# Finishing a LayerNorm with two fused VectorE operations in place of three engines' work, in a hybrid DeltaNet and retention layer

## Chip, core and metric

The kernel runs on one core of one Trainium2 chip. The core's engines are TensorE (PE in the profile, its weight loads PEld), VectorE (DVE), ScalarE (ACT), GpSimd (POOL) and SyncE (SP), which issues every transfer of this kernel. The metric is the time of one execution on the device, in microseconds (us). Three runs of the kernel before took 1587.22 to 1591.74 us, with a median of 1589.14.

## What is computed

The reference is one layer of a diffusion backbone over 1152 tokens of 1024 channels: 128 context tokens and 1024 latent tokens. A mixer with two head groups (gated DeltaNet and retention) is followed by an output projection, a first LayerNorm over the residual, a modulated second LayerNorm, a squared-ReLU MLP and a last LayerNorm. The lines that matter here:

```python
def layer_norm(x, w=None, b=None, eps=1e-6):
    xf = x.astype(jnp.float32)
    mu = jnp.mean(xf, -1, keepdims=True)
    var = jnp.mean(jnp.square(xf - mu), -1, keepdims=True)
    y = (xf - mu) * lax.rsqrt(var + eps)
    if w is not None:
        y = y * w.astype(jnp.float32) + b.astype(jnp.float32)
    return y.astype(x.dtype)
...
        x = layer_norm(ALPHA * x + g1 * y, ln1_w[l], ln1_b[l])
        h = layer_norm(x) * (1.0 + sc2) + sh2
        f = jnp.einsum('btf,fd->btd', jnp.square(jax.nn.relu(jnp.einsum('btd,df->btf', h, w_ff1[l]) + b_ff1[l])),
                       w_ff2[l]) + b_ff2[l]
        x = layer_norm(ALPHA * x + g2 * f, ln2_w[l], ln2_b[l])
```

The first of these norms, with `ln1_w` and `ln1_b`, is the one that the change touches. It is called the first norm below; the plain norm of the next line is the second norm.

## The kernel before

Tokens are worked on in nine tiles of 128 rows. Matrix products are made in three passes: each operand is split into a high part (a cast on ScalarE, line 160) and a low part (a subtraction on VectorE, line 161), and TensorE adds up high by high, high by low and low by high.

The program goes through the input projection, the two scans, the output projection, the MLP's first product, its second product, and the last norm. The change lies in the output projection. Its steps are written as small functions, and a string gives their order (`OPS`, then `FFS`); each letter is a function and each number a tile's place in the order (4, 5, 3, 6, 7, 8, 2, 1, 0). A mark such as `^2500` lets a step's instructions count as that much earlier when the program is ordered. Instructions are put into each engine's queue by a scheduler from priorities and its own times, and each engine then works through its queue in order.

- `L` is `op_load` (line 1067 on): it loads the mixer's output of one tile into `wr` tiles, of which there are two, and splits it (lines 160 and 161).
- `M` is `op_mm`: TensorE multiplies by the output weights (line 1011). For the first six tiles half of the product was made earlier, so `op_mm` has 24 matmuls of 512 columns there and 48 for the last three. VectorE multiplies the PSUM result by the gate (line 1092). For the first six tiles the sum is added to the residual by VectorE for one half and by GpSimd for the other (line 1094); for the last three VectorE does it in one operation (line 1096).
- `A` is `norm1`, the first norm: `stats` (VectorE, lines 245 to 249, then a power on GpSimd for the reciprocal root, line 157), `act_normalise` (a 128x1 product on GpSimd, line 254, and scale and shift on ScalarE, line 255), times the weight on VectorE (line 1103), plus the bias on GpSimd (line 1104), and a store to X1 in device memory, which is read again only near the end of the kernel.
- `B` is `norm2`, the second norm, from the same tile in SBUF: `stats` and `act_normalise` into one of two `n2` tiles.
- `C` is `modulate`: TensorE transposes `n2` (line 1120), ScalarE modulates it out of PSUM into one of two `tmp` tiles (line 1124), the split follows, and `tmp` is stored to HX.
- `F` in `FFS` runs a part of the MLP's first product early (line 194), from the chunks of tokens that are ready.

The small tile `mv` of `stats` holds, in its columns, the mean, the variance plus epsilon, minus the mean (column 2, by line 248) and the reciprocal root (column 3, by line 157). `act_normalise` overwrites column 2 with minus the mean times the root. In the trace the first six tiles of `norm1` appear under the name hL and the last three under r, `mv` as lnmv, and `n2` as n.

Of the kernel before, what the change touches and what calls it, by code (L numbers as in the profile page):

```python
# [12 lines left out]
ALU = mybir.AluOpType  # L13
# [67 lines left out]
def layer_kernel(ctx: ExitStack, tc: tile.TileContext, A, O):  # L81
    nc = tc.nc
    V, S, G, T = nc.vector, nc.scalar, nc.gpsimd, nc.tensor

    def dma(out, in_):
        nc.sync.dma_start(out=out, in_=in_)
# [18 lines left out]
    def pool(name, side="left", **kw):  # L105
        p = tc.tile_pool(name=name, bufs=1, reuse_waits="tile", **(kw or dict(side=side)))
        e = ExitStack()
        p = e.enter_context(p)
        return p, e.close
# [43 lines left out]
    def sb(pool, shape, tag, bufs=1, dt=F32):  # L153
        return pool.tile(shape, dt, tag=tag, name=tag, bufs=bufs)

    def rsqrt(pool, out, in_, n):
        G.tensor_tensor(out=out, in0=in_, in1=ex[:, 0, 0:n], op=ALU.pow)  # L157
# [82 lines left out]
    def stats(pool, x, n, eps):  # L240

        h = n // 512
        st = sb(pool, [128, 2, 6], "lnst", 2)
        for j in range(h):
            V.bn_stats(out=st[:, j, :], in_=x[:, 512 * j:512 * j + 512])  # L245
        mv = sb(pool, [128, 4], "lnmv", 4)
        V.bn_aggr(out=mv[:, 0:2], in_=st[:, 0:h, :])
        V.tensor_scalar(out=mv[:, 2:3], in0=mv[:, 0:1], scalar1=-1.0, scalar2=None, op0=ALU.mult)
        V.tensor_scalar(out=mv[:, 1:2], in0=mv[:, 1:2], scalar1=eps, scalar2=None, op0=ALU.add)  # L249
        rsqrt(pool, mv[:, 3:4], mv[:, 1:2], 1)  # L250
        return mv

    def act_normalise(pool, out, x, mv):
        G.tensor_tensor(out=mv[:, 2:3], in0=mv[:, 2:3], in1=mv[:, 3:4], op=ALU.mult)
        S.activation(out=out, in_=x, func=AF.Identity, scale=mv[:, 3:4], bias=mv[:, 2:3])
# [801 lines left out]
    op, close_op = pool("op")  # L1057
# [3 lines left out]
    l1w = sb(op, [128, 1024], "l1w")  # L1061
    dma(l1w, A["ln1_w"].to_broadcast([128, 1024]))
    l1b = sb(op, [128, 1024], "l1b")
# [35 lines left out]
    def norm1(i):  # L1099
        t = ORDER[i]  # L1100
        r = rt[i]
        act_normalise(op, r, r, stats(op, r, 1024, 1e-6))
        V.tensor_tensor(out=r, in0=r, in1=l1w, op=ALU.mult)
        G.tensor_tensor(out=r, in0=r, in1=l1b, op=ALU.add)
        dma(X1[128 * t:128 * t + 128], r)

    def norm2(i):
# [23 lines left out]
    n2 = {}  # L1131
    HX = dram.tile([1024, NT], F32, name="HX")
    run(OPS, dict(L=op_load, M=op_mm, A=norm1, B=norm2, C=modulate))
    close_ow()

# [29 lines left out]
    def ff1_early(i):  # L1165
# [3 lines left out]
        ff1_chunk(early[f], f, c)  # L1169

    run(FFS, dict(A=norm1, B=norm2, C=modulate, F=ff1_early))
    close_op()
    close_psum()
# [382 lines left out]
```

## Time and profile before

| | |
|---|---|
| median of three runs | 1589.14 us |
| the profiled execution's own time | 1597.36 us |
| its span, first to last instruction | 1595.5 us |
| TensorE matmuls, busy | 1507.1 us, 94% |
| VectorE, busy | 1057.4 us, 66% |
| ScalarE, busy | 724.6 us, 45% |
| GpSimd, busy | 333.4 us, 21% |
| mean granted TensorE clock | 0.977 |

Durations of single instructions come from one profiled execution. The page of the profile gives the busy time of each engine, the span in 40 slices, and the chain of work that ended last. The trace behind it also answers with timelines of one engine (start, duration, engine, line, operation, result and operands, and in brackets the idle time before it and what ended it), with tables of windows, and with groups of instructions: their total, the mean in ns, and the idle time just before them. PE's busy time is modelled from pipelined matmuls, so a full row does not mean that they run at their peak.

### The profile page before, as it was taken

To read this page: it belongs to the slowest core of one execution; us is meant where nothing else is said; L and a number is where in the kernel's file an instruction comes from. 1 tells how busy PE (TensorE), PEld (TensorE's weight loads), DVE (VectorE), ACT (ScalarE), POOL (GpSimd) and SP (SyncE) were. 2 spreads that over 40 slices of the span, in tenths; PEclk is the share of its full clock that TensorE was granted. 3 is DMA by queue.
4 is the path that set the end of the run, shared out by engine and by line. 5 is a ranking of instruction groups with operands and counts; after the bars stand their busy time and mean duration, and the time that the engine had idled before them with its cause. 6 is when DMAs were issued, how large, how long until landed. Compare 5 with 4: busy or idle time off the path is not lost.

```text
span 1595.5 us, 26235 instructions
## 1 busy us (share of the span) xinstructions
PE 1507.1 (94%) x9597; PEld 1328.6 (83%) x9597; DVE 1057.4 (66%) x2045; ACT 724.6 (45%) x1562; POOL 333.4 (21%) x328
## 2 busy tenths in 40 slices
PE   4899999899999999999798999999999999999997
PEld 2697676898898989987687999999998788888885
DVE  4415424568795788657894576656666887867887
ACT  4522312564564464352457565445554453443411
POOL 2201021211112022100541035556553000000000
PEclk9799999999999999999898999999999999999998
DMA  9233556332323123454345944443347989878511
GB/s 347 74 82 83 172 157 200 77 78 70 82 49 102 37 58 108 122 163 161 104 152 158 292 154 139 154 155 128 125 139 260 333 281 315 290 237 284 169 54 66
DMA packets 227378, 247.81 MB, mean 155 GB/s; under 512 B 35956, under 2 KB 161889, under 8 KB 227121
## 3 DMA queue, kind: packets, MB, share of 16 engines
q1 hardware_dynamic: 227249, 246.13, 48.5%
q8 instruction: 76, 1.25, 0.3%
q14 instruction: 53, 0.43, 0.1%
HBM read 185.72 MB, written 56.15 MB: 152 GB/s over the span
## 4 chain that ended last, share of the span: by engine, by line
PE 51%; DVE 10%; issue 4%; ACT 3%; DMA 2%; POOL 2%; SPq 0%; DVEq 0%; POOLq 0%; ACTq 0%
PE d L1252 18%; PE m L1416 14%; PE mm L194 7%; PE d L194 3%; PE p L1416 2%; DVE lnst L245 2%; PE c L900 1%; PE c L891 1%; PE c L884 1%; DVE qk L638 1%; PE co L915 1%; PE co L914 1%; DVE wl L161 1%; DVE acc L1491 1%; POOL lnmv L157 1%
## 5 line engine op out<-in xcount | busy, mean ns | idle before, releaser
L194 PE MATMUL mm<-hH,wh 128*128 128x384 f32 x696 | 247.4, 356 | 2.0 <-ACT raw L634 2.0
L194 PE MATMUL mm<-hL,wh 128*128 128x384 f32 x696 | 246.6, 354 | 0.0
L194 PE MATMUL mm<-hH,wl 128*128 128x384 f32 x696 | 245.7, 354 | 0.0
L161 DVE TENSOR_TENSOR wl<-wr,wh 128x512 fp32r<-128x512 f32 (+1 forms) x149 | 126.8, 855 | 118.3 <-ACT wh L160 109.4
L1416 PE MATMUL m<-vh,sh 128*128 128x512 f32 x460 | 180.6, 393 | 3.4 <-DVE af L1308 3.0
L1416 PE MATMUL m<-vl,sh 128*128 128x512 f32 x460 | 179.8, 393 | 1.4 <-DVE vl L161 1.3
L1416 PE MATMUL m<-vh,sl 128*128 128x512 f32 x460 | 179.6, 391 | 0.4 <-DVE sl L161 0.4
L194 PEld LDWEIGHTS mm<-hH,wh 128*128 128x128 f32 x696 | 133.9, 192 | 7.3 <-ACT raw L634 2.2
L194 PEld LDWEIGHTS mm<-hL,wh 128*128 128x128 f32 x696 | 133.5, 192 | 5.5 <-issue 4.1
L194 PEld LDWEIGHTS mm<-hH,wl 128*128 128x128 f32 x696 | 133.4, 192 | 4.9 <-issue 3.7
L160 ACT CAST wh<-wr 128x512 fp32r<-128x512 f32 (+1 forms) x149 | 88.9, 613 | 78.8 <-PE mm L194 52.2
L1252 PE MATMUL d<-sh,wl 128*128 128x288 f32 x416 | 122.9, 295 | 0.5 <-DVE wl L161 0.5
L1252 PE MATMUL d<-sh,wh 128*128 128x288 f32 x416 | 122.7, 295 | 0.6 <-ACT wh L160 0.6
L1252 PE MATMUL d<-sl,wh 128*128 128x288 f32 x416 | 122.6, 295 | 0.0
L160 ACT CAST sh<-ar 128x512 fp32r<-128x512 f32 x103 | 63.8, 619 | 94.1 <-PE m L1416 46.1
L1416 PEld LDWEIGHTS m<-vh,sh 128*128 128x128 f32 x460 | 86.7, 189 | 22.9 <-issue 3.8
L157 POOL TENSOR_TENSOR lnmv<-lnmv,ex 128x1 f32<-128x1 f32 x36 | 22.0, 612 | 396.4 <-DVE lnmv L249 379.4
L1416 PEld LDWEIGHTS m<-vl,sh 128*128 128x128 f32 x460 | 86.5, 188 | 20.9 <-DVE vl L161 2.1
L1416 PEld LDWEIGHTS m<-vh,sl 128*128 128x128 f32 x460 | 86.8, 189 | 19.1 <-DVE sl L161 0.8
L161 DVE TENSOR_TENSOR sl<-ar,sh 128x512 fp32r<-128x512 f32 x103 | 70.7, 688 | 33.6 <-ACT sh L160 27.6
L1252 PE MATMUL d<-hH,wh 128*128 128x288 f32 x312 | 91.5, 294 | 0.0
L160 ACT CAST vh<-br 128x512 fp32r<-128x512 f32 x103 | 63.8, 619 | 48.9 <-DVE br L1380 32.2
(394 smaller groups left out, 3677.1 us busy)
## 6 DMA issues: line engine op xcount, KB each, us to landing
br<-in_w_ff_dram SPq DMA_DIRECT2D x168, 256.0 KB
ar<-HS SPq DMA_DIRECT2D x91, 256.0 KB
HS<-hL SPq DMA_DIRECT2D x65, 256.0 KB
wm<-in_w_mod_dram SPq DMA_DIRECT2D x32, 512.0 KB
wr<-in_w_in_dram SPq DMA_DIRECT2D x56, 256.0 KB
af<-HX SPq DMA_DIRECT2D x20, 576.0 KB
wm<-in_w_mod_dram SPq DMA_DIRECT2D x8, 1024.0 KB
w3h<-in_w_ff_dram SPq DMA_DIRECT2D x13, 512.0 KB
```

What stands on the lines that cost most here:

```text
L157: G.tensor_tensor(out=out, in0=in_, in1=ex[:, 0, 0:n], op=ALU.pow)
L160: S.copy(out=pool_hi, in_=src)
L161: V.tensor_tensor(out=pool_lo, in0=src, in1=pool_hi.bitcast(F32), op=ALU.subtract)
L194: T.matmul(p[:, 0:384], x[:, k % 4, :], y[c][:, k, :], start=(k == 0 and a == 0), stop=(k == 7 and a == 2),)
L245: V.bn_stats(out=st[:, j, :], in_=x[:, 512 * j:512 * j + 512])
L638: V.scalar_tensor_tensor(out=y, in0=raw[:, tap:tap + 1156], scalar=vec2[:, 12 * tap + ct:12 * tap + ct + 1], in1=y, op0=ALU.mult, op1=ALU.add,
L884: T.matmul(p[:, 0:128], qk[:, 0, off(n):off(n) + 128], old, start=True, stop=True)
L891: T.matmul(p[:, 0:128], UP[:, m_, 0, :], r, start=True, stop=True)
L900: T.matmul(p[:, 0:128], kt[:, n, :], y2, start=True, stop=True)
L914: T.matmul(p[:, 128:256], qk[:, 1, off(n):off(n) + 128], old, start=True, stop=True)
L1252: T.matmul(p[:, q, :], w[x][:, k, :], hs[y][:, k, CH * q:CH * q + CH], start=(k == 0 and a == 0), stop=(k == 3 and a == 2),)
L1416: T.matmul(p, x[i], w[j], start=(first and a == 0), stop=(last and a == 2))
```

## The change

The first norm no longer calls `act_normalise`. After `stats`, one VectorE operation adds minus the mean and multiplies by the weight, and a second one multiplies by the reciprocal root and adds the bias. The 128x1 product on GpSimd, the ScalarE pass, the VectorE product and the GpSimd addition of the first norm are gone; the statistics, the power on GpSimd and the store to X1 stay. The second norm is as it was.

```diff
     def norm1(i):
         t = ORDER[i]
         r = rt[i]
-        act_normalise(op, r, r, stats(op, r, 1024, 1e-6))
-        V.tensor_tensor(out=r, in0=r, in1=l1w, op=ALU.mult)
-        G.tensor_tensor(out=r, in0=r, in1=l1b, op=ALU.add)
+        mv = stats(op, r, 1024, 1e-6)
+        V.scalar_tensor_tensor(out=r, in0=r, scalar=mv[:, 2:3], in1=l1w, op0=ALU.add, op1=ALU.mult)
+        V.scalar_tensor_tensor(out=r, in0=r, scalar=mv[:, 3:4], in1=l1b, op0=ALU.mult, op1=ALU.add)
         dma(X1[128 * t:128 * t + 128], r)
```

## The prediction

> **What bounds the kernel now.** I read the page first, then the chain of waits, then the engines' timelines in the stretch that the chain led to, and last a table of windows. The page gives TensorE 94% of the span, so a change on three other engines can only matter where TensorE stands still. The first `norm1` starts its statistics near 757 us and the last of its work is over by 874 us, so these are the windows I asked for:
>
> ```profile
> core 0: us, PE busy (x) PEld busy (x) DVE busy (x) ACT busy (x) POOL busy (x), PEclk, DMA share, GB/s
> 756.00:874.00 118.00, 100.73 (x481) 86.17 (x480) 86.97 (x154) 67.80 (x133) 46.58 (x51) 0.93 0.42 134
> 779.00:787.00 8.00, 0.07 (x1) 0.07 (x2) 7.80 (x11) 4.65 (x11) 5.03 (x4) 0.65 0.47 145
> 779.00:838.00 59.00, 49.55 (x229) 41.27 (x230) 53.65 (x91) 33.88 (x66) 28.04 (x31) 0.91 0.48 150
> 838.00:874.00 36.00, 28.40 (x151) 26.69 (x150) 16.61 (x30) 28.43 (x64) 5.95 (x8) 0.90 0.48 152
> 874.00:1217.00 343.00, 341.81 (x2475) 341.11 (x2473) 216.93 (x250) 186.76 (x296) 154.37 (x113) 1.00 0.50 168
> ```
>
> TensorE lacks 17.3 us of the 118 in this stretch, 8 of them in one piece, and from 874 on it is busy 341.8 of 343 us. What is won before 874 should therefore reach the end one for one, unless a later transfer has a time of its own. In the piece of 59 us VectorE is busy 53.65, which is 91%: it stands next in line as a bound, and the change puts work on it. TensorE's own waits add up to the same 17.2:
>
> ```profile
> PE s L1120 <- ACT n L255: 8.2, 1, 8.2
> PE d L194 <- ACT tmp L1124: 3.8, 1, 3.8
> PE c L1120 <- ACT tmp L1124: 3.7, 1, 3.7
> PE co L1120 <- DVE r L1092: 1.5, 1, 1.5
> ```
>
> The chain of waits shows how the longest one comes about. Here `norm1` of one tile holds up `norm2` of the tile ahead of it, whose transposes TensorE has next in its queue:
>
> ```profile
> 770.88 0.19 POOL lnmv L254
> ...
> 774.25 2.41 POOL hL L1104
> 776.66 0.97 POOL lnmv L157
> ...
> 777.92 1.25 ACT hL L255
> 779.20 1.24 DVE hL L1103
> ...
> 780.50 0.77 POOL hL L1104
> ...
> 782.80 1.58 POOL hL L1094
> 784.38 0.96 POOL lnmv L157
> ...
> 785.64 1.24 ACT n L255
> ```
>
> The second tile has its mean and scale at 771.07, and its first norm is whole only at 776.66, after ScalarE, VectorE and GpSimd in turn. Its second norm then needs one 128x1 power on GpSimd, which queues behind the next tile's L1104 and L1094 until 784.38; the normalised tile is there at 786.88. GpSimd is 28.04 of 59 us busy, but it is a station that everything passes.
>
> **The change, part by part.** Nine norms each lose a 128x1 multiply on GpSimd (0.19 us, above), a ScalarE pass of 1.25, a VectorE multiply and a GpSimd add, and get two VectorE operations over 128x1024:
>
> ```profile
> L1103 DVE TENSOR_TENSOR hL<-hL,l1w 128x1024 f32<-128x1024 f32 x6 | 7.3, 1222 | 3.7 <-ACT hL L255 3.7
> L1103 DVE TENSOR_TENSOR r<-r,l1w 128x1024 f32<-128x1024 f32 x3 | 3.7, 1226 | 3.2 <-ACT r L255 3.2
> L1104 POOL TENSOR_TENSOR hL<-hL,l1b 128x1024 f32<-128x1024 f32 x6 | 15.1, 2518 | 13.4 <-DVE hL L1103 13.4
> ...
> L1096 DVE SCALAR_TENSOR_TENSOR r<-gx,r x3: 1226/1226/2716, 813.9 to 840.6; 128x1024 f32<-128x1024 f32 x3
> ```
>
> The new form, with a scalar per partition, has no row at this size. The nearest is L1096, the same operation with a constant scalar at the same shape: 1.226 us undisturbed, 2.716 at worst. I take 1.226. VectorE so does one full pass more per norm: 9 x 1.226 = 11.0 us added.
>
> What comes back to VectorE is larger than it looks. Several of its operations on two operands in SBUF take far longer than their own price, and each long one begins while a GpSimd operation runs (the third and the last three rows are GpSimd's):
>
> ```profile
> L161 DVE TENSOR_TENSOR wl<-wr,wh x12: 512/1216/2901, 755.5 to 837.0; 128x512 fp32r<-128x512 f32 x7, 128x384 fp32r<-128x384 f32 x5
> ...
> L161 DVE TENSOR_TENSOR hL<-tmp,hH x10: 669/677/1780, 784.9 to 844.9; 128x512 fp32r<-128x512 f32 x10
> ...
> L157 POOL TENSOR_TENSOR lnmv<-lnmv,ex x18: 546/550/1007, 759.5 to 857.6; 128x1 f32<-128x1 f32 x18
> ...
> 774.88 2.33 DVE L1094 TENSOR_TENSOR hL<-hL,gx 128x512 f32<-128x512 f32 x1
> ...
> 781.13 3.80 DVE L161 TENSOR_TENSOR wl<-wr,wh 128x384 fp32r<-128x384 f32 x2
> ...
> 796.51 2.29 DVE L161 TENSOR_TENSOR wl<-wr,wh 128x512 fp32r<-128x512 f32 x1
> ...
> 806.88 2.57 DVE L161 TENSOR_TENSOR wl<-wr,wh 128x384 fp32r<-128x384 f32 x1
> ...
> 813.90 2.72 DVE L1096 SCALAR_TENSOR_TENSOR r<-gx,r 128x1024 f32<-128x1024 f32 x1
> ...
> 823.76 3.50 DVE L161 TENSOR_TENSOR wl<-wr,wh 128x512 fp32r<-128x512 f32 x2
> ...
> 836.44 3.49 DVE L161 TENSOR_TENSOR wl<-wr,wh 128x512 fp32r<-128x512 f32 x2
> ...
> 795.47 2.78 POOL L1104 TENSOR_TENSOR hL<-hL,l1b 128x1024 f32<-128x1024 f32 x1 [1.84 <-DVE hL L1103]
> ...
> 806.65 2.38 POOL L1104 TENSOR_TENSOR hL<-hL,l1b 128x1024 f32<-128x1024 f32 x1 [1.81 <-DVE hL L1103]
> ...
> 836.60 2.77 POOL L1104 TENSOR_TENSOR r<-r,l1b 128x1024 f32<-128x1024 f32 x1 [1.69 <-DVE r L1103]
> ```
>
> A split of 512 columns alone is 0.68 and one of 384 is 0.51. The excess under L1104 is 2.33 - 0.68 = 1.65; 1.7 of the pair at 781.13 (until L1094 begins at 782.80; the rest is L1094's and stays); 2.29 - 0.68 = 1.6; 2.57 - 0.51 = 2.06; 2.72 - 1.23 = 1.5; and twice 3.5 - 1.36 = 2.1. Together 12.8 us, which goes if L1104 goes. The waits ahead of L1103 for ScalarE, 3.7 + 3.2 = 6.9 us, go as well, since the first new operation needs only the mean, which VectorE itself has just written.
>
> One wait is added: the second new operation needs the power of L157 from GpSimd. Behind it in VectorE's queue stand evictions (L1092) and splits, on which TensorE and the loads live. Alone, a power takes 0.55 us and would lie under the 1.23 us of the first operation. Two rows say that it will not: the power at 776.66 ends at 777.63, 0.42 after the L1094 that began at 774.88 ends (777.21), and the one at 784.38 ends at 785.34, 0.41 after the splits of 781.13 end (784.93). A power that meets a VectorE operation with two SBUF operands is finished only 0.4 us behind it. The new first operation is of that kind and starts first, so I charge 0.5 us of waiting per norm (0.4 and a hand-over), 4.5 for nine; the other end is nothing. The Trainium skill says the same as a rule that speaks against the change ("SBUF — State Buffer", section Who interferes with whom): a VectorE instruction with two SBUF inputs and a GpSimd instruction that reads SBUF exclude each other, and the second to issue blocks fully until the first is done. By that rule the power hides behind nothing and the sum is 1580.1, without it 4.5 us of VectorE's time less; the rows just named agree with it.
>
> VectorE's balance is then +11.0 + 4.5 - 12.8 - 6.9 = -4.2 us. If VectorE's order decided everything, the stretch would shrink by 4.2.
>
> TensorE could take more. The tile whose first norm was whole at 776.66 now needs two operations and 0.5 of waiting, some 3.0 us in place of 5.6 (771.07 to 776.66): 2.6 won. From there to 782.80 the chain runs through the next tile's first norm, which loses its ScalarE pass, 1.25, and its L1104, 2.3 (780.50 to 782.80). That makes 6.1 of the 8.2; the whole 8.2 goes if VectorE also takes the second norm's statistics ahead of the next tile, and that is the upper end. After that wait TensorE also runs slowly for a while:
>
> ```profile
> 789.13 0.63 PE L1011 MATMUL co<-woh,wl 128*128 128x512 f32 x1
> 789.55 0.63 PE L1011 MATMUL co<-wol,wh 128*128 128x512 f32 x1
> ...
> 793.07 0.39 PE L1011 MATMUL s<-woh,wl 128*128 128x512 f32 x1
> 793.30 0.40 PE L1011 MATMUL s<-wol,wh 128*128 128x512 f32 x1
> ```
>
> Starts lie 0.42 us apart at 789 and 0.23 at 793; over the some eight matmuls and the transposes ahead of them that is about 2.2 us (the granted clock is 0.65 in the window of the wait), and it goes with the wait. So TensorE's view is 8.2 + 2.2 + 1.5 for the wait on L1092, whose queue is rid of the long splits, 11.9 in all; and of the 3.7 before L1120 perhaps everything, since these ScalarE steps wait for a `tmp` tile that VectorE's splits and a store behind the X1 store on SP's queue set free. That is 15.6 at most. The last wait of 3.8 I leave: ScalarE is 28.43 of 36 us busy in that window, nearly all of it modulation, and it loses there two or three passes of 1.25 that were not the last to end.
>
> The X1 store is the same transfer on the same queue; it becomes ready some 3 us sooner, and what SP has behind it (HX stores, weight loads) with it.
>
> Between 4.2 and 15.6 I take 9.0: nearer to the lower end, as VectorE at 91% follows TensorE only as far as its own balance allows. The profiled execution took 1597.36 us (its span is 1595.5, with 1.9 around it), 8.2 above the median of the runs, 1589.14. I subtract the 9.0 from both: 1588.4 for a profiled execution like this one, 1580.1 for the median.
>
> **The rivals.** *All of it goes.* TensorE loses its waits as in the upper sum, and the power hides after all, or the last wait shrinks too: 14 to 18 us, about 1573. For it: the longest wait is a queueing accident at one place. Against it: VectorE's 91%. Chance 0.12.
>
> *Given back further on.* The wait at 787 goes, and TensorE arrives early at the heavier steps that follow, where each half of the activations is loaded into one of two `wr` tiles, cast and split before it can be used. At 806.88 that split ran 2.57 us and ended at 809.45, as the matmuls that use it came up; there may be no slack. Then only some of the 4.2 stays: 0 to 5 us, about 1587. For it: the loads depend on VectorE and SP, not on TensorE. Against it: that split was itself one of the stretched ones. Chance 0.22.
>
> *Slower: VectorE becomes the bound.* Its extra 11.0 + 4.5 come in full, but the 12.8 do not come back, because the new operations and splits now fall under the L1094 adds, which stay on GpSimd, or because the long rows have another cause. Less the 6.9 this is +8.6 for nine norms; six of them lie in the window that is 91% full, so 5.7 reach the end: 1594.8. It decides from the point at which less than two thirds (8.6 of 12.8) return. Against it: seven of seven long rows lie over a GpSimd add. For it: L1094 shows at 782.80 that it stretches too. Chance 0.16.
>
> **How the numbers follow.** The forecast, 5 to 14 us saved, has 0.50. A measurement of this kernel tells about 0.3% from no change, 4.8 us. Faster by more: 0.50 + 0.12 + 0.04 of the second rival = 0.66. Slower by more: 0.14 of the third rival's 0.16. The same: the remaining 0.18 and 0.02, 0.20. The range: the lower end takes in most of the first rival, 18 us, 1571; the upper end takes in the second rival whole and the mild half of the third, 1591.5. The forecast's own range is 1575 to 1584.
>
> **What would show it.** Right: TensorE's wait for n at L1120 is under 2 us and the matmuls behind it run at full pace; no split over 2 us except under L1094; in VectorE's rows a gap near 0.5 us ahead of the second new operation; VectorE's busy time in the stretch within 3 us of 86.97; the 874 mark at about 865. Wrong: the stretched splits are still there though L1104 is gone; or new waits of TensorE on a split or on L1092 sum to more than 5 us; or the mark at 874 moves and the end does not.

## The result, and the profile after

The changed kernel took 1581.17 us in the median of eight runs, the kernel before 1590.44 beside it on the same chips. The ratio is 0.9939 with a 95% interval of 0.9917 to 0.9960: 9.7 us saved, 6.3 to 13.2. One execution of the kernel before took 3743 us; the ratio leaves it out and so isn't that of the two medians. The unaltered kernel run once more among the experiments gave 0.9937 (0.9915 to 0.9959).

Single profiles differ by more than that, and not where the change is. The first GpSimd addition at L1094 starts at 756.74 us in the profile of before and at 741.88 in the profile after, though up to there both programs are the same; over the thirteen profiles of this study that have this addition on GpSimd, that mark lies between 741.9 and 759.4. Whole spans of two profiles therefore can't be set against each other. What can be is the stretch from that mark to the first L194 matmul into a `d` tile. These are the windows of that stretch, before and after (columns as in the prediction: length, busy time of PE, PEld, DVE, ACT and POOL, the granted clock, DMA):

```profile
756.74:873.52 116.78, 99.51 (x477) 85.08 (x475) 86.32 (x152) 67.32 (x132) 46.57 (x51) 0.93 0.43 135
```

```profile
741.88:847.76 105.88, 96.27 (x476) 81.45 (x474) 84.17 (x161) 58.53 (x123) 28.22 (x33) 0.98 0.46 150
```

The stretch is 10.9 us shorter. In the repeat it is 104.99 us (749.77 to 854.76), so the stretch repeats within 0.9 us where the span does not. From its end to the end of the span it is 722.0 us before, 724.8 after and 725.9 in the repeat: nothing further is won there. It is 2.9 and 3.9 us longer, so that single profiles save 8.0 and 7.8 us from the mark to the end; why it is longer is open. In the stretch VectorE is busy 2.15 us less although it does nine passes more. TensorE's waits after are these (total, times, longest):

```profile
PE c L1120 <- ACT n L255: 4.0, 2, 2.5
PE d L194 <- ACT tmp L1124: 3.8, 1, 3.8
PE co L1011 <- DVE wl L161: 1.3, 1, 1.3
PE c L194 <- DVE hL L161: 0.3, 1, 0.3
PE c L194 <- ACT hH L160: 0.2, 1, 0.2
```

They sum to 9.6 us, from 17.2. That is 7.6 of the 10.9. The other 3.2 are TensorE's busy time, 99.51 us before and 96.27 after for 477 and 476 matmuls: the granted clock in the two windows is 0.93 and 0.98. In the repeat TensorE is busy 94.83 us, at 1.00. The wait of 8.2 has become two of 4.0 together, 3.7 and 1.5 are gone, the last of 3.8 has stayed, and a wait on a split, 1.3, is new. Where VectorE's time went is in its groups of the same stretch after:

```profile
L245 DVE BATCH_NORM_STATS2 lnst<-hL 128x6 f32<-128x512 f32 x23 | 14.8, 670 | 1.4 <-POOL hL L1094 1.4
L161 DVE TENSOR_TENSOR hL<-tmp,hH 128x512 fp32r<-128x512 f32 x17 | 12.5, 737 | 15.2 <-ACT hH L160 15.1
L1104 DVE SCALAR_TENSOR_TENSOR hL<-hL,lnmv,l1b 128x1024 f32<-128x1024 f32 x6 | 8.7, 1449 | 0.3 <-POOL lnmv L157 0.3
...
L1103 DVE SCALAR_TENSOR_TENSOR hL<-hL,lnmv,l1w 128x1024 f32<-128x1024 f32 x6 | 7.6, 1262 | 0.0
L161 DVE TENSOR_TENSOR wl<-wr,wh 128x512 fp32r<-128x512 f32 x7 | 5.5, 784 | 0.3 <-ACT wh L160 0.2
...
L1104 DVE SCALAR_TENSOR_TENSOR r<-r,lnmv,l1b 128x1024 f32<-128x1024 f32 x3 | 3.8, 1277 | 0.0
L1103 DVE SCALAR_TENSOR_TENSOR r<-r,lnmv,l1w 128x1024 f32<-128x1024 f32 x3 | 3.8, 1261 | 0.0
L1096 DVE SCALAR_TENSOR_TENSOR r<-gx,r 128x1024 f32<-128x1024 f32 x3 | 3.6, 1212 | 0.0
...
L1094 DVE TENSOR_TENSOR hL<-hL,gx 128x512 f32<-128x512 f32 x5 | 3.4, 672 | 0.0
...
L161 DVE TENSOR_TENSOR wl<-wr,wh 128x384 fp32r<-128x384 f32 x4 | 2.2, 572 | 0.0
```

The same groups of old operations in the stretch before:

```profile
L245 DVE BATCH_NORM_STATS2 lnst<-hL 128x6 f32<-128x512 f32 x23 | 15.0, 676 | 4.2 <-POOL hL L1094 2.9 <-POOL hL L1104 1.3
L161 DVE TENSOR_TENSOR hL<-tmp,hH 128x512 fp32r<-128x512 f32 x17 | 12.6, 748 | 15.3 <-ACT hH L160 15.3
L161 DVE TENSOR_TENSOR wl<-wr,wh 128x512 fp32r<-128x512 f32 x7 | 11.7, 1697 | 0.0
...
L161 DVE TENSOR_TENSOR wl<-wr,wh 128x384 fp32r<-128x384 f32 x4 | 5.8, 1438 | 0.0
L1096 DVE SCALAR_TENSOR_TENSOR r<-gx,r 128x1024 f32<-128x1024 f32 x3 | 5.2, 1723 | 0.1
L1094 DVE TENSOR_TENSOR hL<-hL,gx 128x512 f32<-128x512 f32 x5 | 5.0, 1003 | 0.0
```

The two kinds of splits, L1096 and L1094 cost VectorE 11.7 + 5.8 + 5.2 + 5.0 = 27.7 us before and 5.5 + 2.2 + 3.6 + 3.4 = 14.7 after, for equal counts: 13.0 us back. All four read two operands in SBUF. The statistics of L245, which read one, take the same before and after (676 and 670 ns). The new pair costs 23.9 us where L1103 alone cost 7.3 + 3.7 = 11.0.

VectorE also stands still less. In the kernel before it waited, besides the 6.9 us ahead of L1103, for GpSimd ahead of the statistics:

```profile
DVE lnst L245 <- POOL hL L1094: 2.9, 2, 1.5
DVE lnst L245 <- POOL r L1104: 2.5, 1, 2.5
DVE lnst L245 <- POOL hL L1104: 1.3, 1, 1.3
```

After, only 1.4 us ahead of the statistics (on L1094) and 0.3 ahead of L1104 are left of all these. I call **held** the time that VectorE's queue stands still for such a station of the norm: 6.9 + 2.9 + 2.5 + 1.3 = 13.6 us before, 1.7 after. Busy and held together are 99.9 us before and 85.9 after. Held leaves out VectorE's other waits, above all the 15 us that it waits in both kernels for ScalarE's casts ahead of the splits into `hL`.

### The profile page after: what moved, and what is told of

Same layout as the page of the kernel before. It is cut to its first block, busy times and chain, and to the rows that moved or that the text cites. A ratio compares the mean times of both kernels' runs of the same rounds, so it can differ in the third digit from the quotient of the medians.

```text
span 1572.6 us, 26198 instructions
## 1 busy us (share of the span) xinstructions
PE 1494.0 (95%) x9597; PEld 1316.9 (84%) x9597; DVE 1056.6 (67%) x2054; ACT 715.8 (46%) x1553; POOL 314.9 (20%) x310
## 4 chain that ended last, share of the span: by engine, by line
PE 52%; DVE 9%; issue 4%; DMA 3%; ACT 3%; POOL 2%; SPq 0%; DVEq 0%; POOLq 0%; ACTq 0%
PE d L1252 16%; PE m L1416 15%; PE mm L194 7%; PE d L194 2%; PE p L1416 2%; DVE lnst L245 2%; PE s L1011 1%; PE c L900 1%; PE c L884 1%; PE c L891 1%; DVE qk L638 1%; PE co L915 1%; PE co L914 1%; DVE acc L1491 1%; DVE acc L1498 1%
## 5 line engine op out<-in xcount | busy, mean ns | idle before, releaser
L194 PE MATMUL mm<-hH,wh 128*128 128x384 f32 x696 | 246.2, 354 | 2.2 <-ACT raw L634 2.2
L194 PE MATMUL mm<-hL,wh 128*128 128x384 f32 x696 | 245.1, 352 | 0.0
L194 PE MATMUL mm<-hH,wl 128*128 128x384 f32 x696 | 244.3, 351 | 0.0
L161 DVE TENSOR_TENSOR wl<-wr,wh 128x512 fp32r<-128x512 f32 (+1 forms) x149 | 117.1, 789 | 115.1 <-ACT wh L160 109.8
L194 PEld LDWEIGHTS mm<-hH,wh 128*128 128x128 f32 x696 | 132.6, 191 | 7.9 <-ACT raw L634 2.4
L194 PEld LDWEIGHTS mm<-hL,wh 128*128 128x128 f32 x696 | 132.6, 191 | 5.8 <-issue 4.1
L194 PEld LDWEIGHTS mm<-hH,wl 128*128 128x128 f32 x696 | 132.4, 190 | 4.9 <-issue 3.7
L157 POOL TENSOR_TENSOR lnmv<-lnmv,ex 128x1 f32<-128x1 f32 x36 | 25.8, 716 | 417.9 <-DVE lnmv L249 403.1
L1252 PE MATMUL d<-hH,wh 128*128 128x288 f32 x312 | 91.5, 294 | 0.0
```

The lines of the kernel that those rows point to most:

```text
L161: V.tensor_tensor(out=pool_lo, in0=src, in1=pool_hi.bitcast(F32), op=ALU.subtract)
L194: T.matmul(p[:, 0:384], x[:, k % 4, :], y[c][:, k, :], start=(k == 0 and a == 0), stop=(k == 7 and a == 2),)
L1252: T.matmul(p[:, q, :], w[x][:, k, :], hs[y][:, k, CH * q:CH * q + CH], start=(k == 0 and a == 0), stop=(k == 3 and a == 2),)
```

## The experiments

The changed kernel was run once more beside them, unaltered.

> The changed kernel unaltered, to see how far one profile of it lies from another. The stretch from the first L1094 addition on GpSimd to the first L194 matmul into d took 116.8 us in the kernel before and 105.9 in the changed kernel. If the stretch depends on the order of the queues and not on the execution, it is 105 to 107 again, and the runs are 5 to 12 us under the kernel before.

The ratio of 0.9937 and the stretch of 104.99 us, both above, are what was expected.

The theories at the outset. A: the GpSimd addition is what cost, by its place in the tile's chain and by the VectorE rows it stretches. B: the ScalarE pass and its hand-overs cost. C: VectorE's time is the bound. All ratios are to the kernel before, from five rounds; "stretch" is the one above.

**The bias addition alone moved to VectorE.**

```diff
-        G.tensor_tensor(out=r, in0=r, in1=l1b, op=ALU.add)
+        V.tensor_tensor(out=r, in0=r, in1=l1b, op=ALU.add)
```

> The kernel before with one edit: the bias addition of the first norm on VectorE; the ScalarE pass and the 128x1 product stay. The changed kernel is at 0.9939 of the kernel before (9.7 us). Theory A, that the GpSimd addition is what costs (its 2.4 us in each chain, and the splits it stretches): this edit alone saves 5 to 8 us, and no split over 2 us is left except under L1094. Theory B, that the ScalarE pass and the hand-overs to and from it cost: 0 to 3 us saved, since VectorE gets 9 x 1.23 us more and the chain keeps three engines' stations. Theory C, VectorE as the bound: within 2 us of the kernel before.

Ratio 0.9973 (0.9947 to 0.9999), stretch 112.4 us (748.01 to 860.44). That is 4.4 of the 10.9, between A's and B's figures. The long splits are gone as A says, but VectorE stands still ahead of L1103 for 8.0 us (6.9 before):

```profile
DVE hL L1103 <- ACT hL L255: 5.6, 5, 2.4
DVE lnst L245 <- POOL hL L1094: 3.0, 3, 1.4
DVE r L1103 <- ACT r L255: 2.4, 3, 1.4
```

**The second operation taken apart, GpSimd adding the bias again.**

```diff
-        V.scalar_tensor_tensor(out=r, in0=r, scalar=mv[:, 3:4], in1=l1b, op0=ALU.mult, op1=ALU.add)
+        V.tensor_scalar(out=r, in0=r, scalar1=mv[:, 3:4], scalar2=None, op0=ALU.mult)
+        G.tensor_tensor(out=r, in0=r, in1=l1b, op=ALU.add)
```

> The changed kernel with the second fused operation taken apart: VectorE scales by the reciprocal root, GpSimd adds the bias as in the kernel before. The ScalarE pass and the 128x1 product stay gone. Theory A: the GpSimd addition brings the stretched splits and its queue back, 0 to 3 us saved against the kernel before, seven or so VectorE rows over 2 us. Theory B: 6 to 9 us saved. Theory C: VectorE has the added pass (of one operand, perhaps cheaper) and the stretched rows both, so slower than the kernel before by 0 to 6 us.

Ratio 1.0003 (0.9975 to 1.0031), stretch 117.6 (751.95 to 869.51): everything is lost again, with the ScalarE pass still gone. B falls as a cause by itself. The stretched rows are back, for instance

```profile
786.29 2.90 DVE L161 TENSOR_TENSOR wl<-wr,wh 128x512 fp32r<-128x512 f32 x1
...
818.63 2.70 DVE L161 TENSOR_TENSOR wl<-wr,wh 128x512 fp32r<-128x512 f32 x1
```

VectorE is busy 89.2 us and held 8.9.

**A further VectorE pass, off the tile's chain and on it.**

```diff
+        V.scalar_tensor_tensor(out=l1w, in0=l1w, scalar=1.0, in1=l1w, op0=ALU.mult, op1=ALU.max)   # off the chain
+        V.scalar_tensor_tensor(out=r, in0=r, scalar=1.0, in1=r, op0=ALU.mult, op1=ALU.max)         # on it, in another kernel
```

> The changed kernel with one further VectorE pass over 128x1024 after each first norm, on the weight tile (its maximum with itself), for which no norm of the same tile waits. Theory A, in which VectorE has some room again once the stretched rows are gone: 0 to 4 us slower than the changed kernel. Theory C, VectorE as the bound: the full pass, 7 to 11 us slower than the changed kernel, so about the kernel before.

> The same further pass of 1.23 us, but on the norm's own tile (its maximum with itself), so that the store and the second norm wait for it. Theory A, that the chain of one tile sets TensorE's waits: 2 to 6 us slower than the changed kernel and more than the pass off the chain, with a longer wait of TensorE ahead of L1120. Theory C: as off the chain, 7 to 11 us, without a difference between the two.

Off the chain: ratio 0.9986 (0.9960 to 1.0012), stretch 114.1 (753.02 to 867.14), 8.2 more than 105.9. On it: 0.9968 (0.9944 to 0.9991), stretch 115.6 (744.94 to 860.51), 9.7 more. This is C's figure in both stretches. By the ratios the two are 7.5 and 4.6 us slower than the changed kernel; the second is A's figure, and with intervals of some 4 us to either side the ratios can't tell the two kernels apart. C rests on the stretches here. The nine passes are 11.0 us; VectorE's busy time rises by 8.4 off the chain and 9.2 on it, as other rows are shorter. Off the chain TensorE waits for what stands behind the pass in the queue:

```profile
L1105 DVE SCALAR_TENSOR_TENSOR l1w<-l1w 128x1024 f32<-128x1024 f32 x9 | 11.0, 1218 | 0.0
```

```profile
PE mm L194 <- DVE wl L161: 5.4, 1, 5.4
...
PE co L1011 <- DVE wl L161: 2.4, 1, 2.4
```

**The wait for the power taken away.** This kernel leaves out the scaling of the first norm.

```diff
-        V.scalar_tensor_tensor(out=r, in0=r, scalar=mv[:, 3:4], in1=l1b, op0=ALU.mult, op1=ALU.add)
+        V.scalar_tensor_tensor(out=r, in0=r, scalar=1.0, in1=l1b, op0=ALU.mult, op1=ALU.add)
```

> The changed kernel with the constant 1.0 in place of the reciprocal root in the second fused operation: it leaves out the scaling of the first norm, and with it VectorE's wait for the power; the power itself is still computed. The prediction charged 0.5 us of VectorE's waiting per norm, 4.5 in all: by it the stretch is 2 to 4.5 us shorter than 105.9. The trace of the changed kernel shows only one such wait, of 0.3 us, with other VectorE work between the two operations: by that, 104.5 to 106.5.

Ratio 0.9958 (0.9930 to 0.9986), stretch 107.5 (754.13 to 861.65). That is outside both figures: not shorter but 1.6 to 2.5 longer, and VectorE's queue has another order in the later norms. Nothing like the 4.5 us came of taking the wait away.

**GpSimd's addition back, but off the chain of its tile.** The next tile's second operation reads `l1b` and comes behind the addition; in the trace VectorE never waits for that. `zero` is a column of zeros in the `op` pool.

```diff
+        G.tensor_tensor(out=l1b, in0=l1b, in1=zero[:, 0:1].to_broadcast([128, 1024]), op=ALU.add)
```

> The changed kernel with a GpSimd addition of 128x1024 (zero added to the bias tile) after each first norm, for which the tile's own store and second norm do not wait. Theory A1, that the GpSimd addition costs by what it stretches on VectorE and by its place in GpSimd's queue ahead of the powers: the stretched splits are back, and the stretch is 112 to 118 us. Theory A2, that it costs because the tile's own chain waits for it: 105 to 109, stretched splits or not.

Ratio 0.9991 (0.9972 to 1.0009), stretch 114.2 (754.86 to 869.01): A1. It costs 8.3 us although nothing of the tile waits for it. The three VectorE groups that lengthen, and TensorE's longest wait:

```profile
L161 DVE TENSOR_TENSOR hL<-tmp,hH 128x512 fp32r<-128x512 f32 x17 | 14.8, 878 | 14.8 <-ACT hH L160 14.8
...
L1098 DVE SCALAR_TENSOR_TENSOR r<-gx,r 128x1024 f32<-128x1024 f32 x3 | 5.3, 1764 | 0.0
...
L1096 DVE TENSOR_TENSOR hL<-hL,gx 128x512 f32<-128x512 f32 x5 | 4.6, 917 | 0.0
```

```profile
PE c L1123 <- ACT n L255: 7.3, 2, 4.1
```

(L1098 and L1096 are here what L1096 and L1094 are elsewhere.) VectorE's busy time rises from 84.2 to 89.2 us, without one instruction more on it: the three groups take 2.3, 1.7 and 1.2 us more than in the changed kernel. The splits into `wl`, the long ones of the kernel before, are not longer here (5.5 and 2.2 us, as in the changed kernel). On TensorE's side the 8.3 us are 5.3 more of waiting, 3.3 of them for `n`, and 2.9 more busy time, at a granted clock of 0.96. The powers for `n` stand behind the additions in GpSimd's queue; how much comes of that and how much of the longer VectorE rows was not measured apart.

**ScalarE's load put back, off the chain and on it.**

```diff
+        S.activation(out=l1b, in_=l1b, func=AF.Identity)   # off the chain
+        S.activation(out=r, in_=r, func=AF.Identity)       # on it, in another kernel
```

> The changed kernel with a ScalarE pass over 128x1024 (the bias tile copied onto itself) after each first norm, for which the tile's own store and second norm do not wait: ScalarE's old load and place in its queue, without the hand-over. If ScalarE's time costs as GpSimd's does, the stretch is 111 to 116 us in place of 105 to 106; if the ScalarE pass cost only by the hand-over in the tile's chain, 105 to 108.

> The changed kernel with a ScalarE pass of 1.25 us on the norm's own tile (copied onto itself), for which the store and the second norm wait; the counterpart of the ScalarE pass off the chain, which gave 106.7 us. If ScalarE's old pass cost by its place in the chain, as the run with the bias addition on VectorE (112.4) suggests: 110 to 113. If that run's 112.4 has another cause (the 128x1 product on GpSimd, or another order of the queues): 106 to 108.

Off the chain: ratio 0.9935 (0.9899 to 0.9971), stretch 106.7 (759.44 to 866.13). On the chain: 0.9920 (0.9889 to 0.9951), stretch 104.2 (756.10 to 860.26). Neither costs, and the second lies below both figures of its expectation: a ScalarE pass in the tile's chain is free when it stands behind VectorE's operations. In the first experiment, where it stands ahead of them, the stretch is 6.5 us longer (112.4 against 105.9); there the 128x1 product on GpSimd stands ahead of them too, and the two were not taken apart. VectorE's waits point the same way. Of the pass behind them it notices

```profile
DVE lnst L245 <- ACT r L1105: 0.3, 1, 0.3
```

and of the two stations ahead of them, in the first experiment, 8.0 us. By these stretches the part of A that reads the chain of one tile falls.

**Three attempts to go further.** The second norm on VectorE as well; the six L1094 halves of GpSimd on VectorE; and the seventh and eighth tile's modulation earlier in the order.

```diff
-        act_normalise(op, n2[i], r, stats(op, r, 1024, 1e-6))
+        mv = stats(op, r, 1024, 1e-6)
+        V.tensor_scalar(out=n2[i], in0=r, scalar1=mv[:, 2:3], scalar2=mv[:, 3:4], op0=ALU.add, op1=ALU.mult)
...
-                (G if j else V).tensor_tensor(out=r[:, js], in0=r[:, js], in1=y[:, js], op=ALU.add)
+                V.tensor_tensor(out=r[:, js], in0=r[:, js], in1=y[:, js], op=ALU.add)
...
-FFS = "F11 F01 A8 B7 B8^2500 F12 F02 C7 F21 C6^150 C8^6000 F22"
+FFS = "F11 F01 A8 C6^1000 B7 B8^2500 F12 C7^1000 F02 F21 C8^6000 F22"
```

> The changed kernel with the second norm finished in the same manner: one VectorE operation (add minus the mean, multiply by the reciprocal root) in place of the 128x1 product on GpSimd and the ScalarE pass. VectorE gets nine passes of one operand, 0.74 us each in the run with the scale on VectorE, 6.7 in all. Theory A (chain): two stations and their hand-overs fewer ahead of TensorE's transposes, the stretch 101 to 105 us. Theory C (VectorE as the bound): 108 to 113.

> The changed kernel with the six L1094 half additions that GpSimd still does moved to VectorE too, 6 x 0.68 = 4.1 us more for VectorE. Nothing is left that stretches VectorE's rows (2.3 and 1.6 us in the changed kernel, about 2 us of excess together) or delays the powers. If GpSimd as a station is what costs: the stretch is 102 to 105 us. If VectorE's time is by now the currency: 106 to 109.

> The changed kernel with the order string FFS changed, so that the modulation of the seventh and eighth tile is given out ahead of the early matmuls and not behind them; all the same work. The prediction left the last wait of 3.8 us ahead of the d matmuls alone, as ScalarE's modulation fills the 14 us before it. If that is because three tiles' modulation is bunched there, behind TensorE's early matmuls in its queue, the wait goes and the stretch is 2 to 4 us shorter (101 to 104). If the last tile alone sets the end: unchanged, 105 to 106.

The second norm on VectorE: ratio 0.9959 (0.9931 to 0.9986), stretch 107.9 (753.09 to 861.02), outside both expectations; VectorE is busy 6.8 us more, and only 2 of it show. The halves: 0.9970 (0.9952 to 0.9989), stretch 109.3 (its first VectorE addition at L1094 is at 750.91, and the mark comes 3.16 behind that in the changed kernel; it ends at 863.39), just outside both figures too. That is 3.4 longer though VectorE's busy time rose by only 0.5 us. TensorE waits 2.7 us more there, 1.3 of it on a split and 1.1 on `tmp`; the cause is open. The order: 0.9958 (0.9934 to 0.9982), stretch 109.6 (747.59 to 857.18), a miss for both expectations. The wait of 3.8 ahead of the `d` matmuls is gone, and another has come ahead of the early ones, because the cast of their weights now stands behind the modulation in ScalarE's queue:

```profile
PE mm L194 <- ACT w3h L160: 5.8, 1, 5.8
```

This stretch can't be set beside the others as it stands. It holds 3.4 us of VectorE work (L1200, L1203 and one split) that the changed kernel does behind its end, and behind its end it is 719.6 us long in place of 724.8. From the mark to the end of the span it takes 829.2 us, the changed kernel 830.7 and its repeat 830.9. So the order is not shown to be worse, nor better.

None of the kernels tried is faster than the changed one beyond its interval.

**All of them by VectorE's account** (us):

| kernel | stretch | busy | held | sum |
|---|---|---|---|---|
| before | 116.8 | 86.3 | 13.6 | 99.9 |
| scale on VectorE, add on GpSimd | 117.6 | 89.2 | 8.9 | 98.1 |
| pass on the chain | 115.6 | 93.4 | 1.4 | 94.8 |
| pass off the chain | 114.1 | 92.6 | 2.0 | 94.6 |
| add alone on VectorE | 112.4 | 83.4 | 11.0 | 94.4 |
| GpSimd off the chain | 114.2 | 89.2 | 2.3 | 91.5 |
| modulation earlier | 109.6 | 87.6 | 1.7 | 89.3 |
| changed | 105.9 | 84.2 | 1.7 | 85.9 |
| changed, repeated | 105.0 | 84.1 | 1.7 | 85.8 |
| ScalarE on the chain | 104.2 | 83.6 | 1.7 | 85.3 |
| ScalarE off the chain | 106.7 | 83.6 | 1.7 | 85.3 |
| no wait for the power | 107.5 | 82.5 | 2.6 | 85.1 |
| halves on VectorE | 109.3 | 84.6 | 0.3 | 84.9 |

The account was drawn up after the runs. Sums near 85 go with stretches of 104 to 110, counting the earlier modulation among them, whose sum is 85.8 without the 3.4 us named above; sums of 91 to 95 go with 112 to 116, sums of 98 to 100 with 117 to 118. Busy time alone would not sort them: the add alone on VectorE has 83.4. But what the sum leaves out of a stretch is just VectorE's other idle time, 17 to 24 us, so the table shows where the time lies and not what set it; the experiments above have to do that. The second norm on VectorE (busy 91.0, held 2.1, stretch 107.9) doesn't fit: there VectorE waits only 8.5 us for ScalarE's casts. The differences of up to 5 us among sums near 85 were not traced to a cause; two executions of the unaltered kernel differ by 0.9 us, and an edit can change the order of the queues, as in the kernel without the wait for the power.

## Why the prediction was right

**Where the time is.** TensorE's standing still between 757 and 874 was the right place: the stretch gave 10.9 us and the rest nothing. That all of it reaches the end, "one for one", isn't what the single profiles show (8.0 and 7.8 us). The forecast of 9.0 met 9.7, with an interval that allows for either.

**What comes back to VectorE.** 12.8 us were read off the stretched rows; 13.0 came back. The cause was not only argued from rows that overlap: the addition on GpSimd, put back with nothing of its tile waiting for it, raised VectorE's busy time by 5.0 us, and taken away alone it ended the long splits.

**The added pass.** 11.0 predicted, 12.9 measured. The operation with a scalar per partition takes 1.23 to 1.29 us, with means of 1.26 and 1.28, and L1096 with a constant 1.20 to 1.23; and one of the eighteen fell under an L1094 addition and took 2.31.

**The wait for the power: the step that failed.** The step said that the power, held behind the first new operation, would make VectorE wait 0.5 us per norm, 4.5 in all. The holding is there, but not the waiting. The first norm after, on VectorE and on GpSimd:

```profile
744.36 1.28 DVE L1103 SCALAR_TENSOR_TENSOR hL<-hL,lnmv,l1w 128x1024 f32<-128x1024 f32 x1
745.57 0.68 DVE L1092 TENSOR_TENSOR gx<-s,g 128x512 f32<-128x512 f32 x1
746.17 1.27 DVE L1104 SCALAR_TENSOR_TENSOR hL<-hL,lnmv,l1b 128x1024 f32<-128x1024 f32 x1
```

```profile
744.61 1.45 POOL L157 TENSOR_TENSOR lnmv<-lnmv,ex 128x1 f32<-128x1 f32 x1 [1.44 <-DVE lnmv L249]
```

The power takes 1.45 us in place of 0.55 and ends at 746.06, 0.42 behind L1103, as the rows of before and the Trainium skill's rule on two SBUF inputs ("SBUF — State Buffer", Who interferes with whom) had it. But the queue has an eviction between the two operations, and by the time L1104 comes up the power is done. In all nine norms other VectorE work stands there. In the third it is only two operations of 128x1, and there VectorE waits 0.3 us, the whole wait of the nine. The rows gave the hold; the order of the queue, which decides whether a hold is a wait, was not in them.

**VectorE's balance.** Predicted -4.2; measured -14.0 (99.9 to 85.9). The power is 4.2 us of the difference, and the waits of the statistics on L1104 and L1094, 3.8 and 1.5 us, were not in the sum at all. The forecast came out near the mark because a balance too small by ten was weighed against TensorE's upper view of 15.6. So far it was luck.

**TensorE's view.** It was worked out as the shortening of one tile's chain. That was the wrong reason: a ScalarE pass put into that chain behind VectorE's work costs nothing. What went with the old stations is VectorE's standing still, 11.9 us of it. The slow spell was sized too small: 2.2 us were charged, and TensorE's busy time fell by 3.2, in the repeat by 4.7. The sum had only the spell behind the wait of 8.2; a second one, behind the wait of 3.7 (a granted clock of 0.77 from 842 to 850 us and 0.81 to 858), is gone too. Of the other terms, 3.7 and 1.5 went, the 8.2 left 4.0 and not nothing, and the last 3.8 stayed as predicted.

**The rivals.** "Slower, as VectorE becomes the bound" had part of the bound right: nine passes more on VectorE cost 8.2 and 9.7 us of the stretch, but the second norm's 6.8 us more cost 2.0. Its price was wrong, since the 12.8 did come back. "Given back further on" happened by 1.3 us on a split (2.0 in the repeat), and by the 2.9 to 3.9 us behind the stretch, which it did not foresee. "All of it goes" needed 14 us; TensorE kept 9.6 us of waiting.

**The signs.** Of the signs of being right, three came: no split takes over 2 us, VectorE's busy time is near its old one, and the mark is earlier, by 10.9 us in place of 9. Two did not: the wait for `n` is 4.0 us and not under 2, with slow matmuls behind it in one of two executions, and there is no gap ahead of the second operation. No sign of being wrong came, as most of what the stretch gave reached the end.

## What to carry to other kernels

Read an engine's waits beside its busy time. The kernel with the add alone on VectorE was busy less than the changed one (83.4 and 84.2 us) and its stretch was 6.5 us longer, as its queue stood still for other engines. Say which waits are counted, since busy time and all waits together are the stretch itself. Here nine GpSimd additions that no later step of their tile waited for raised VectorE's busy time by 5.0 us, in operations that read two operands in SBUF, and a further full VectorE pass per norm paid for itself by removing such additions. A station on another engine cost where VectorE's queue had to stand still for it, and next to nothing where it stood behind VectorE's work.

## What the runs showed of the hardware that was not expected

TensorE's wait of 2.51 us was followed by a slow spell in one execution and not in another of the same program. In the profile after, the second and third matmul behind it start 0.43 us apart, in the repeat 0.23:

```profile
763.64 0.47 PE L1120 MATMUL c<-ident,n 128*128 128x128 f32 x1 [2.51 <-ACT n L255]
...
764.34 0.63 PE L1011 MATMUL s<-woh,wl 128*128 128x512 f32 x1
764.77 0.63 PE L1011 MATMUL s<-wol,wh 128*128 128x512 f32 x1
```

```profile
771.53 0.33 PE L1120 MATMUL c<-ident,n 128*128 128x128 f32 x1 [2.51 <-ACT n L255]
...
771.93 0.40 PE L1011 MATMUL s<-woh,wl 128*128 128x512 f32 x1
772.16 0.40 PE L1011 MATMUL s<-wol,wh 128*128 128x512 f32 x1
```

From the transposition behind the wait to the first product into `co` the same matmuls take 4.97 us in the one, at a granted clock of 0.70, and 3.64 in the other, at 1.00. Of this 1.3 us the repeat gives 0.7 back in a longer wait on a split; the two stretches differ by 0.9.
